# Weight parts stored once and loaded ready-made: a change to a hybrid decoder trunk on one Trainium2 core

## The chip, the cores and the metric

The kernel runs on one core of one Trainium2 chip. The metric is device time in microseconds of one execution, lower is better. The engines are TensorE (PE, with its weight loads as PEld), VectorE (DVE), ScalarE (ACT), GpSimd (POOL) and SyncE (SP), which issues nearly all DMAs of this kernel in program order. Each engine works through its own queue in order, and semaphores tie the queues together.

## The reference

One layer of a decoder trunk, for one prompt of 2048 tokens and 8 samples of 8 tokens (2112 token columns in all). Four recurrent mixers of 256 columns each work side by side between two dense projections, and a squared-ReLU channel mixer follows:

```python
h = rmsnorm(x, p['norm1_w']) * (1 + sc1) + sh1
u = jnp.einsum('btd,de->bte', h, p['w_in'])
u_a, u_b, u_c, u_d = split_last(u, IN_SIZES)
...   # y_a: RWKV-7, y_b: gated linear attention, y_c: gated delta net, y_d: SSD
y = jnp.concatenate([y_a, y_b, y_c, y_d], -1) @ p['w_out']
x = x + gt1 * y
h = rmsnorm(x, p['norm2_w']) * (1 + sc2) + sh2
f = jnp.square(jax.nn.relu(h @ p['w_up'])) @ p['w_down']
x = x + gt2 * f
```

The model width is 1024, the hidden width 4096; `w_in` is padded to 32 column tiles of 128. A last RMSNorm gives the output, and the mixers' states are outputs too.

## The kernel before

**Dense products.** All dense products keep float32 accuracy with three reduced-precision products: weights and activations are split into a high part (the value rounded to the engine's float32r type) and a low part (what is left), and `mm3` (lines 117 to 119) adds hi x hi, hi x lo and lo x hi in PSUM. `wload` makes the weights' parts. It works by half tiles of [128, 512]: a DMA on SP brings the raw half (`wr`, four buffers, line 99), ACT casts it to `wh` (three buffers, line 100), and the subtraction that gives `wl` (three buffers, line 102) runs in turn on GpSimd and DVE, on DVE alone in the two large blocks. A half tile then serves 4 x 3 products for each token tile.

**How often each weight is read.** The input projection (`stage_A`) runs over the tokens in four passes of 320, 2 x 360, 2 x 360 and 352 columns, and reads all 64 half tiles of `w_in` in each. The output projection (`F_out`), the up projection (`F_up`) and the down projection (`F_down`) run over four blocks: two small ones of 352 and 360 columns, numbered 0 and 1, and two large ones of 2 x 350 columns, numbered 2 and 3. `SMALL` is the number of small blocks, 2. Each small block reads 16 half tiles of `w_out`, 64 of `w_up` and 64 of `w_down`. So with one token tile a half serves 12 products, with two it serves 24.

**What runs beside them.** The mixers work on eight chunks of 256 prompt tokens and, once, on the samples. They run in two lanes. Their work is many small operations: short products in PSUM tiles named `psm`, convolutions by `conv_silu` (line 698 on DVE), triangular solves (lines 510 to 543), norms. They read the projected columns `u` back from DRAM (line 1915) and store their results `yd` (line 1922). A scheduler lays out each engine's queue ahead of time: the mixers' instructions come first wherever they are ready, the dense stages fill in. Input passes 1 to 3 and the two small blocks run beside the mixers, the two large blocks after them. So a mixer product that waits on DVE holds up the dense products behind it in PE's queue, and a dense product that waits for a weight part holds up the mixers.

Of the kernel before, what the change touches and what calls it, by code (L numbers as in the profile page):

```python
# [8 lines left out]
F32 = mybir.dt.float32  # L9
# [19 lines left out]
WR, WH, WL = 4, 3, 3  # L29
# [7 lines left out]
class Dense:  # L37
    def __init__(self, es, tc, io):
# [8 lines left out]
        self.a_rstd = {}  # L47
        nc.scalar.preload_act_table_set("exp_and_others")
# [10 lines left out]
    def phase(self, pool, width, temps=4, xs=6, lo_eng=None):  # L59
        """Working tiles of the dense stages come from this pool, `width` tokens wide."""  # L60
        self.sb, self.W, self.temps, self.xs = pool, width, temps, xs
        self.lo_eng = lo_eng or [self.nc.vector]
# [25 lines left out]
    def act(self, tags, w, bufs=1):  # L88
        """High and low parts of activations [128, 8, w]; tags: one each."""
        return [self.sb.tile([128, KT, w], F32R, tag=tag, name=self.n(tag), bufs=bufs) for tag in tags]  # L90

    def wload(self, src):
        """A weight tile in two halves, each as a high and a low part."""
        nc, out = self.nc, []
        for h in range(2):
            raw = self.wp.tile([128, 512], F32, tag="wr", name=self.n("wr"), bufs=WR)
            hi = self.wp.tile([128, 512], F32R, tag="wh", name=self.n("wh"), bufs=WH)
            lo = self.wp.tile([128, 512], F32R, tag="wl", name=self.n("wl"), bufs=WL)
            self.w_dma = nc.sync.dma_start(raw, src[:, h * 512 : h * 512 + 512]).ins.name
            nc.scalar.copy(hi, raw)  # L100
            self.lo_i += 1
            self.lo_eng[self.lo_i % len(self.lo_eng)].tensor_tensor(out=lo, in0=raw, in1=hi.bitcast(F32), op=ALU.subtract)  # L102
            out.append((hi, lo))
        return out

    def after_w(self, dma):
        """Keep a load behind the last weights in the queue."""
# [3 lines left out]
    def mm3(self, ps, w, ks, first=True, last=True):  # L111
        """ps += W^T X from high and low parts: hi*hi + hi*lo + lo*hi."""
# [8 lines left out]
    def project(self, src, xs, tag="d"):  # L121
        """PSUM tiles of W^T X for one column tile of a [1024, .] weight; xs: (n, hi, lo) per token tile."""
        w = self.wload(src)
# [7 lines left out]
    def ada(self, raw, halves, psum, tmp):  # L131
        """Modulation vectors [128, 48, 9]; raw(), halves(): two [128, 512] halves for weights and for sums, psum(): a PSUM tile, tmp: [128, 512]."""
# [22 lines left out]
    def ada_part(self, i):  # L155
        """Weights of input tile i % 8 for the six vectors; each vector is done with its last one. Its input tiles are summed by fours
        in the column groups of the array, whose sums are folded by the products that transpose them."""
# [32 lines left out]
    def rstd_bc(self, s, n):  # L190
        """1/rms per token, on all partitions, from per-partition sums of squares s [128, n]."""
# [25 lines left out]
    def split_cols(self, t0, n):  # L217
        """The sample's columns come first."""
# [22 lines left out]
    def modulate(self, src, r, A, shb, t0, n, hi, lo):  # L241
        """hi + lo = (x / rms) * A + shift, x from DRAM."""
# [24 lines left out]
    def hold(self, tile):  # L267
        """The first tile's input stays on chip."""
# [15 lines left out]
    def stage_A(self, i, store, between):  # L284
        """One pass over the input projection; the next pass's norms are prepared on the way."""
# [9 lines left out]
        for j, ct in enumerate([31] + list(range(31))):  # L295
# [3 lines left out]
            for (t0, n, _, _), ps in zip(acts, self.project(self.io["w_in"][ct], [(n, hi, lo) for _, n, hi, lo in acts])):  # L299
# [11 lines left out]
    def gated_add(self, dst, ps, base, ct, ns, n):  # L311
        """dst += gate * ps, the gate per channel (and per sequence in the sample's columns)."""
# [1855 lines left out]
```

## Time and profile before

| | |
|---|---|
| median of 3 runs | 3463.68 us |
| lowest and highest | 3456.1 and 3464.03 us |
| span of the profiled execution | 3454.3 us |
| mean granted TensorE clock | 0.954 |
| DMA traffic | 411.60 MB, mean 119 GB/s |
| weight half tiles loaded, 256 KB each | 872 |

The profiled execution's own time is given as its span, from the first to the last instruction; the runs' times hold what lies around a span as well. A page's group row reads: line, engine, operation, tiles written and read, shapes, count, then busy microseconds, mean nanoseconds of one, then the engine's idle time just before them and what ended it. A row of waits reads: who waited, for whom, microseconds in total, times, longest. A row by stretch gives for a span of time its length, each engine's busy time with its count, the granted clock, the share of DMA time and the rate. A row of one line's instructions gives the shortest, the median and the longest duration in nanoseconds, and the first and the last start.

### The profile page before, as it was taken

What the parts mean: (1) busy time and instruction counts of PE and PEld (TensorE: products, weight loads), DVE (VectorE), ACT (ScalarE), POOL (GpSimd) and SP (SyncE); (2) the same over time, 40 slices, a digit from 0 to 9 for tenths busy, and PEclk for the clock granted to TensorE, in tenths of its full rate; (3) what the DMA queues carried; (4) which work ended last, traced back from release to release, by engine and by line L of the source; (5) the groups of instructions that cost most, each with busy time, mean ns of one, the idle gap of its engine ahead of it and who ended that gap; (6) DMA issues with size and microseconds to landing.
All of it is one profiled execution on the core that took longest, in us unless ns stands there. A gap on an engine that the chain in (4) does not pass through costs nothing.

```text
span 3454.3 us, 62438 instructions
## 1 busy us (share of the span) xinstructions
PE 3297.9 (95%) x23286; PEld 3024.6 (88%) x23286; DVE 2181.7 (63%) x4739; ACT 1471.0 (43%) x3098; POOL 999.7 (29%) x1034
## 2 busy tenths in 40 slices
PE   8999999899998999999989999997999999999998
PEld 5679887898987988988878888887999999999998
DVE  3437555856668769879879869865334445433345
ACT  3453423434344454454454554544332344332334
POOL 2333334624335346336346336242000000000000
PEclk9999999999999989999988999988999999999999
DMA  9863334423235555333343232355222252222222
GB/s 308 257 188 110 92 100 132 137 82 106 95 104 135 147 127 145 99 113 106 117 129 121 96 121 92 124 156 179 72 68 70 95 192 82 98 68 71 68 70 95
DMA packets 339475, 411.60 MB, mean 119 GB/s; under 512 B 98900, under 2 KB 211684, under 8 KB 339172
## 3 DMA queue, kind: packets, MB, share of 16 engines
q1 hardware_dynamic: 339172, 407.62, 38.2%
q8 instruction: 183, 3.00, 0.4%
q14 instruction: 120, 0.98, 0.1%
HBM read 342.69 MB, written 64.80 MB: 118 GB/s over the span
## 4 chain that ended last, share of the span: by engine, by line
PE 73%; DVE 16%; DMA 4%; issue 3%; ACT 2%; POOL 1%; SPq 1%; DVEq 0%; ACTq 0%; POOLq 0%
PE psd L119 19%; PE psd L118 19%; PE psd L117 19%; DVE t L698 3%; DVE wl L102 2%; PE psm L173 1%; DMA u<-u 1%; DVE Xt L517 1%; DVE X L519 1%; DMA ada<-ada_w 1%; DVE d L248 1%; DVE acc L314 1%; PE pse L118 1%; PE pse L117 1%; PE pse L119 1%
## 5 line engine op out<-in xcount | busy, mean ns | idle before, releaser
L100 ACT CAST wh<-wr 128x512 fp32r<-128x512 f32 x872 | 536.2, 618 | 1049.1 <-PE psd L118 884.6
L119 PE MATMUL psd<-a,wl 128*128 128x360 f32 (+3 forms) x2304 | 783.7, 341 | 26.9 <-DVE wl L102 23.8
L118 PE MATMUL psd<-a,wh 128*128 128x360 f32 (+3 forms) x2304 | 780.4, 339 | 7.2 <-DVE a L257 3.4
L117 PE MATMUL psd<-a,wh 128*128 128x360 f32 (+3 forms) x2304 | 779.3, 339 | 5.3 <-ACT a L253 3.1
L102 DVE TENSOR_TENSOR wl<-wr,wh 128x512 fp32r<-128x512 f32 x584 | 430.5, 738 | 333.6 <-ACT wh L100 325.2
L102 POOL TENSOR_TENSOR wl<-wr,wh 128x512 fp32r<-128x512 f32 x288 | 398.9, 1386 | 704.0 <-ACT wh L100 633.0
L119 PEld LDWEIGHTS psd<-a,wl 128*128 128x128 f32 x2304 | 450.9, 196 | 66.8 <-DVE wl L102 30.5
L117 PEld LDWEIGHTS psd<-a,wh 128*128 128x128 f32 x2304 | 451.1, 196 | 30.2 <-issue 9.6
L118 PEld LDWEIGHTS psd<-a,wh 128*128 128x128 f32 x2304 | 451.0, 196 | 24.2 <-issue 10.0
L314 DVE SCALAR_TENSOR_TENSOR acc<-psd,mod,acc 128x350 f32<-128x350 f32 (+2 forms) x384 | 216.7, 569 | 246.4 <-PE psd L119 245.5
L117 PE MATMUL psd<-hh,wh 128*128 128x350 f32 x1024 | 333.3, 326 | 3.4 <-ACT d L368 3.4
L117 PE MATMUL psd<-fh,wh 128*128 128x350 f32 x1024 | 329.3, 323 | 3.7 <-DVE acc L314 3.7
L118 PE MATMUL psd<-hl,wh 128*128 128x350 f32 x1024 | 332.5, 325 | 0.0
L119 PE MATMUL psd<-fh,wl 128*128 128x350 f32 x1024 | 330.9, 324 | 1.2 <-DVE wl L102 1.0
L119 PE MATMUL psd<-hh,wl 128*128 128x350 f32 x1024 | 331.4, 324 | 0.0
L118 PE MATMUL psd<-fl,wh 128*128 128x350 f32 x1024 | 331.3, 324 | 0.0
L215 POOL TENSOR_TENSOR rsc<-rsc,bias 128x2 f32<-128x2 f32 (+4 forms) x30 | 21.3, 720 | 1004.8 <-ACT rsc L203 1002.7
L117 PEld LDWEIGHTS psd<-hh,wh 128*128 128x128 f32 x1024 | 194.3, 190 | 4.0 <-ACT d L368 4.0
L117 PEld LDWEIGHTS psd<-fh,wh 128*128 128x128 f32 x1024 | 193.0, 189 | 4.7 <-DVE acc L314 4.7
L118 PEld LDWEIGHTS psd<-hl,wh 128*128 128x128 f32 x1024 | 195.2, 191 | 0.1
L119 PEld LDWEIGHTS psd<-hh,wl 128*128 128x128 f32 x1024 | 194.6, 190 | 0.0
L119 PEld LDWEIGHTS psd<-fh,wl 128*128 128x128 f32 x1024 | 192.7, 188 | 1.7 <-DVE wl L102 1.7
(581 smaller groups left out, 5977.8 us busy)
## 6 DMA issues: line engine op xcount, KB each, us to landing
wr<-w_down SPq DMA_DIRECT2D x264, 256.0 KB
wr<-w_in SPq DMA_DIRECT2D x256, 256.0 KB
wr<-w_up SPq DMA_DIRECT2D x256, 256.0 KB
ada<-ada_w SPq DMA_DIRECT2D x96, 256.0 KB
wr<-w_out SPq DMA_DIRECT2D x96, 256.0 KB
u<-uo SPq DMA_DIRECT2D x128, 180.0 KB
u<-u SPq DMA_DIRECT2D x124, 128.0 KB
xp<-xT SPq DMA_DIRECT2D x72, 180.0 KB
```

The source lines that it names most:

```text
L100: nc.scalar.copy(hi, raw)
L102: self.lo_eng[self.lo_i % len(self.lo_eng)].tensor_tensor(out=lo, in0=raw, in1=hi.bitcast(F32), op=ALU.subtract)
L117: nc.tensor.matmul(ps, lhsT=lh, rhs=xh, start=first and i == 0, stop=False)
L118: nc.tensor.matmul(ps, lhsT=lh, rhs=xl, start=False, stop=False)
L119: nc.tensor.matmul(ps, lhsT=ll, rhs=xh, start=False, stop=last and i == len(ks) - 1)
L173: nc.tensor.matmul(ps[h][o : o + 32], lhsT=self.cT[:, k], rhs=w[h], start=(k < 4), stop=(k >= 4))
L215: self.nc.gpsimd.tensor_tensor(out=ap, in0=ap, in1=e.to_broadcast(list(ap.shape)), op=ALU.pow)
L248: nc.vector.scalar_tensor_tensor(out=t[:, ns:n], in0=x[:, ns:n], scalar=A[:, k, 0:1], in1=r[:, ns:n], op0=ALU.mult, op1=ALU.mult)
L314: nc.vector.scalar_tensor_tensor(out=dst[:, ns:n], in0=ps[:, ns:n], scalar=self.mod[:, base + ct, 0:1], in1=dst[:, ns:n], op0=ALU.mult, op ...
L517: nc.vector.tensor_tensor(out=tmp[:, :n, :w], in0=X[:, a:hi, j : j + 1].to_broadcast([128, n, w]), in1=MM[:, j, lo:j].unsqueeze(1).to_broa ...
L519: nc.vector.tensor_tensor(out=X[:, a:hi, lo:j], in0=X[:, a:hi, lo:j], in1=tmp[:, :n, :w], op=ALU.add)
L698: nc.vector.scalar_tensor_tensor(out=y[:, q], in0=uv[:, q, i : i + n], scalar=w(i), in1=y[:, q], op0=ALU.mult, op1=ALU.add)
```

## The change

The high and the low part of a half tile become one tile `w` of [128, 2, 512] with three buffers, in place of `wh` and `wl` with three each. `wload` takes a key. The first time that it meets a key, it makes the two parts as before and then stores the tile, 512 KB, to DRAM; the next times it loads that tile into a `w` buffer in one DMA, with no raw half, no cast and no subtraction. Without a key all is as before.

Keys are given to the input projection in passes 1 to 3 (stored in pass 1, loaded in 2 and 3) and to the output, up and down projections in blocks 0 and 1 (stored in 0, loaded in 1). Pass 0 and the two large blocks have none. That is 64 + 16 + 64 + 64 = 208 stores and 128 + 16 + 64 + 64 = 272 ready-made loads.

```diff
-WR, WH, WL = 4, 3, 3
+WR, WB = 4, 3
...
+        self.kept = {}
...
-    def wload(self, src):
+    def wload(self, src, key=None):
         nc, out = self.nc, []
+        kept = self.kept.get(key)
+        made = []
         for h in range(2):
-            raw = self.wp.tile([128, 512], F32, tag="wr", name=self.n("wr"), bufs=WR)
-            hi = self.wp.tile([128, 512], F32R, tag="wh", name=self.n("wh"), bufs=WH)
-            lo = self.wp.tile([128, 512], F32R, tag="wl", name=self.n("wl"), bufs=WL)
-            self.w_dma = nc.sync.dma_start(raw, src[:, h * 512 : h * 512 + 512]).ins.name
-            nc.scalar.copy(hi, raw)
-            self.lo_i += 1
-            self.lo_eng[self.lo_i % len(self.lo_eng)].tensor_tensor(out=lo, in0=raw, in1=hi.bitcast(F32), op=ALU.subtract)
-            out.append((hi, lo))
+            w = self.wp.tile([128, 2, 512], F32R, tag="w", name=self.n("w"), bufs=WB)
+            if kept is not None:
+                self.w_dma = nc.sync.dma_start(w.bitcast(F32), kept[h]).ins.name
+            else:
+                raw = self.wp.tile([128, 512], F32, tag="wr", name=self.n("wr"), bufs=WR)
+                self.w_dma = nc.sync.dma_start(raw, src[:, h * 512 : h * 512 + 512]).ins.name
+                nc.scalar.copy(w[:, 0], raw)
+                self.lo_i += 1
+                self.lo_eng[self.lo_i % len(self.lo_eng)].tensor_tensor(out=w[:, 1], in0=raw, in1=w[:, 0].bitcast(F32), op=ALU.subtract)
+                if key is not None:
+                    d = self.dram.tile([128, 2, 512], F32, name=self.n("wk"))
+                    nc.sync.dma_start(d, w.bitcast(F32))
+                    made.append(d)
+            out.append((w[:, 0], w[:, 1]))
+        if made:
+            self.kept[key] = made
         return out
...
-    def project(self, src, xs, tag="d"):
-        w = self.wload(src)
+    def project(self, src, xs, tag="d", key=None):
+        w = self.wload(src, key)
...
-            ... self.project(self.io["w_in"][ct], [(n, hi, lo) for _, n, hi, lo in acts])
+            ... self.project(self.io["w_in"][ct], [(n, hi, lo) for _, n, hi, lo in acts], key=("in", ct) if i else None)
...
-                ps, = self.project(self.io["w_out"][ct], [(n, hi, lo)], "e")
+                ps, = self.project(self.io["w_out"][ct], [(n, hi, lo)], "e", ("out", ct) if bi < SMALL else None)
...
-            ... self.project(self.io["w_up"][cc * 4 + j], hs)
+            ... self.project(self.io["w_up"][cc * 4 + j], hs, key=("up", cc * 4 + j) if bi < SMALL else None)
...
-            w = self.wload(self.io["w_down"][cc, c2])
+            w = self.wload(self.io["w_down"][cc, c2], ("down", cc, c2) if bi < SMALL else None)
```

What this does to the queues is shown at three places. The first is SP's queue at the start of block 0's channel mixer, where the accumulator `acc` is loaded. Before (line 99 loads a raw half, line 1922 stores a mixer's result):

```order
L392 DMA acc_20000<-x2d 128x8x352
L99 DMA wr_20093<-w_up 128x512
L1901 DMA u_5_259<-uo_17447 128x352
L1905 DMA u_p<-uo_17447 128x3
L99 DMA wr_20129<-w_up 128x512
L99 DMA wr_20135<-w_up 128x512
L1922 DMA yd_269<-yN_12689 128x2x256
L99 DMA wr_20171<-w_down 128x512
L99 DMA wr_20177<-w_down 128x512
```

Now (line 104 loads a raw half, line 110 stores a made tile `w` to its place `wk` in DRAM):

```order
L403 DMA acc_19504<-x2d 128x8x352
L110 DMA wk_19519<-w_19514 128x1024
L1912 DMA u_5_259<-uo_16951 128x352
L1916 DMA u_p<-uo_16951 128x3
L110 DMA wk_19556<-w_19551 128x1024
L104 DMA wr_19603<-w_up 128x512
L104 DMA wr_19640<-w_up 128x512
L110 DMA wk_19563<-w_19558 128x1024
L104 DMA wr_19647<-w_up 128x512
```

Each raw load has a store of twice its size beside it, and the store of a half stands behind its own raw load and three later ones, since it waits for the subtraction.

The second is SP's queue in block 1, a little behind the load of its accumulator. Before (line 1915 loads a mixer's columns `u`):

```order
L99 DMA wr_23574<-w_down 128x512
L1915 DMA u_17983<-u_4_144 128x160
L1915 DMA u_17983<-u_5_145 128x96
L1915 DMA u_17983<-u_4_150 128x160
L1915 DMA u_17983<-u_5_151 128x96
L99 DMA wr_23608<-w_down 128x512
L99 DMA wr_23614<-w_down 128x512
```

Now (line 101 loads a ready-made tile, line 1926 a mixer's columns):

```order
L101 DMA w_23066<-wk_19695 128x1024
L101 DMA w_23096<-wk_19736 128x1024
L1926 DMA u_18324<-u_5_103 128x256
L1926 DMA u_18324<-u_5_109 128x256
L1926 DMA u_18334<-u_5_115 128x256
L1926 DMA u_19288<-u_5_217 128x256
L1926 DMA u_19288<-u_5_223 128x256
L101 DMA w_23098<-wk_19743 128x1024
```

The load of a weight now goes straight into the buffer that PE reads and waits for PE's last product on that buffer; the mixers' loads stand between such loads.

The third is PE's queue around the mixers' last product. Before, it stands in the output projection of block 2 (350 columns), with 8332 of the 14976 dense products ahead of it:

```order
L119 MATMUL psd_26642<-a_4776_26247,wl_26632 128x350
L117 MATMUL psd_26642<-a_4776_26247,wh_26631 128x350
L713 MATMUL psm_19741<-ident,u_19738 128x128 x4
L118 MATMUL psd_26642<-a_4777_26248,wh_26631 128x350
L119 MATMUL psd_26642<-a_4776_26247,wl_26632 128x350
```

Now it stands in the up projection of block 1 (360 columns), with 7546 ahead:

```order
L130 MATMUL psd_24320<-a_3820_22823,w_24316 128x360
L128 MATMUL psd_24320<-a_3820_22823,w_24316 128x360
L724 MATMUL psm_19245<-ident,u_19242 128x128 x4
L129 MATMUL psd_24320<-a_3821_22824,w_24316 128x360
L130 MATMUL psd_24320<-a_3820_22823,w_24316 128x360
```

786 dense products have moved from beside the mixers to behind them.

More of the change, by code (lines that the diff above doesn't have):

```diff
@@ L298, in stage_A @@
                 self.norm_A(*A_PASSES[i + 1][j == 22])
-            for (t0, n, _, _), ps in zip(acts, self.project(self.io["w_in"][ct], [(n, hi, lo) for _, n, hi, lo in acts])):
+            for (t0, n, _, _), ps in zip(acts, self.project(self.io["w_in"][ct], [(n, hi, lo) for _, n, hi, lo in acts], key=("in", ct) if i else None)):
                 o = self.d2("uo", 2)
@@ L364, in F_up @@
             fh, fl = ftile(j)
-            for (t0, n), ps in zip(tiles, self.project(self.io["w_up"][cc * 4 + j], hs)):
+            for (t0, n), ps in zip(tiles, self.project(self.io["w_up"][cc * 4 + j], hs, key=("up", cc * 4 + j) if bi < SMALL else None)):
                 o = t0 - b0
```

## The prediction

> **What bounds the kernel now.** I read the page first (busy shares, slices, chain), then the busy times by stretch, then who waits for whom.
>
> ```profile
> span 3454.3 us, 62438 instructions
> PE 3297.9 (95%) x23286; PEld 3024.6 (88%) x23286; DVE 2181.7 (63%) x4739; ACT 1471.0 (43%) x3098; POOL 999.7 (29%) x1034
> PE 73%; DVE 16%; DMA 4%; issue 3%; ACT 2%; POOL 1%; SPq 1%; DVEq 0%; ACTq 0%; POOLq 0%
> ```
>
> PE is busy 95% of the span and carries 73% of the chain that ended last; VectorE (DVE) has the next 16%. PE's work stays what it is, so the change can only move the 156 us in which PE is idle, and the time that PE spends at a lower granted clock. Where these lie:
>
> ```profile
> core 0: us, PE busy (x) PEld busy (x) DVE busy (x) ACT busy (x) POOL busy (x), PEclk, DMA share, GB/s
> 0.00:240.00 240.00, 228.04 (x1256) 157.82 (x1256) 93.06 (x207) 100.12 (x216) 78.42 (x109) 1.00 0.79 256
> 240.00:635.00 395.00, 385.62 (x2841) 342.94 (x2840) 253.82 (x675) 154.51 (x365) 151.29 (x169) 0.95 0.41 114
> 635.00:1060.00 425.00, 411.99 (x3362) 374.55 (x3361) 291.50 (x692) 183.48 (x405) 156.28 (x173) 0.96 0.35 105
> 1060.00:1310.00 250.00, 230.45 (x1794) 206.50 (x1792) 190.41 (x436) 116.40 (x253) 113.41 (x112) 0.92 0.54 138
> 1310.00:1790.00 480.00, 451.39 (x3510) 408.37 (x3507) 414.51 (x979) 235.69 (x499) 228.97 (x216) 0.93 0.38 119
> 1790.00:2370.00 580.00, 530.04 (x3955) 478.32 (x3954) 469.78 (x958) 279.72 (x587) 252.35 (x236) 0.90 0.38 123
> 2370.00:3454.00 1084.00, 1060.40 (x6580) 1056.12 (x6580) 468.58 (x798) 401.08 (x776) 19.01 (x23) 0.99 0.27 90
> ```
>
> The rows are about the stages: input passes 0, 1, 2 and 3 (the last with the first block's output projection), channel mixer of block 0, of block 1, and of the two large blocks. I call **lost** the idle time of PE plus its busy time times the missing clock. Passes 1 and 2 lose 9.4 + 0.05 x 385.6 = 29 us and 13.0 + 0.04 x 412.0 = 29 us, 7% of each, with DVE busy 64% and 69%. The next three lose 19.6 + 18.4 = 38 (15%, DVE 76%), 28.6 + 31.6 = 60 (13%, DVE 86%) and 50.0 + 53.0 = 103 us (18%, DVE 81%). The last stretch is nearly all PE, and its weights take the same route as before: nothing to win there.
>
> **What the change takes away.** Of the 872 half tiles, 272 are now loaded ready-made: 128 in input passes 2 and 3, and 16 + 64 + 64 of the output, up and down projections of block 1. Each drops a cast and a subtraction, the latter in turn on DVE and GpSimd (POOL):
>
> ```profile
> L100 ACT CAST wh<-wr 128x512 fp32r<-128x512 f32 x872 | 536.2, 618 | 1049.1 <-PE psd L118 884.6
> L102 DVE TENSOR_TENSOR wl<-wr,wh 128x512 fp32r<-128x512 f32 x584 | 430.5, 738 | 333.6 <-ACT wh L100 325.2
> L102 POOL TENSOR_TENSOR wl<-wr,wh 128x512 fp32r<-128x512 f32 x288 | 398.9, 1386 | 704.0 <-ACT wh L100 633.0
> ```
>
> That is 272 x 0.618 = 168 us of ACT, 136 x 0.738 = 100 us of DVE and 136 x 1.386 = 188 us of POOL. None of it is PE time, so what counts is PE's wait for it, by the waits of PE in 1060:1310 and then in 1790:2370, the two kept stretches with losses:
>
> ```profile
> PE psd L119 <- DVE wl L102: 5.3, 3, 3.0
> ```
> ```profile
> PE psd L119 <- DVE wl L102: 11.0, 9, 3.7
> PE pst L334 <- DMA yp<-yd: 6.7, 5, 1.8
> PE psd L334 <- DMA xp<-yd: 6.2, 6, 2.3
> ```
>
> That is 16.3 us directly. More comes through the mixers: their chains run on DVE, and PE, which takes its queue in order, waits for them. By the table the loss goes from 7% at a DVE share of 69% to about 15% at 81% (the mean of three), 0.68% for each point. In 1790:2370 DVE loses 72 x 0.738 = 53 us and goes from 81% to 72%: 6.1% of 580 is 35 us. In 1060:1310 it loses 32 x 0.738 = 24 us, 76% to 67%: 15 us. Pass 2 is at 7% already: nothing. Of these 50 us, which include the 16.3, I take off the quarter that the two loads of y (12.9 of the 50 idle us of block 1) make up, which stay: **38 us gained**. Bounds: 16 us (the waits on wl alone) and 59 us (both stretches down to 7%).
>
> The order shows the same: behind the mixers' last product stand 786 more dense products than before. The cast's release moves from the second to the third product of a weight tile (one tile now holds both parts), 0.16 us by the starts below; the half tiles in front of it cover that, and with the cover gone it would be 0.16 us a half tile.
>
> **What the kept loads cost.** A ready-made half is 128 x 1024 values, 512 KB, into one of three buffers, issued only when PE has let the buffer go; before, four raw halves lay loaded ahead of three made pairs. The pace of the dense products, 24 starts apart, and loads of 256 KB in the chain:
>
> ```profile
> 2319.78 0.32 PE L118 MATMUL psd<-a,wh 128*128 128x350 f32 x1
> ...
> 2323.69 0.33 PE L118 MATMUL psd<-f,wh 128*128 128x360 f32 x1
> ```
> ```profile
> 1256.07 4.23 DMA wr<-w_in
> 2004.34 2.11 DMA wr<-w_down
> ```
>
> 3.91 / 24 = 0.163 us a product, so a half tile of 12 lasts PE 1.96 us. The trace gives no time for such a load of 512 KB of weights. From the tail's 90 GB/s at a share of 0.27 (333 GB/s at full share) the second 256 KB adds 0.79 us: between 2.9 and 5.0 us. With 0.33 us to issue,
>
> ```profile
> L99 SPq DMA_DIRECT2D wr<-w_down x264: 327/328/1312, 1328.6 to 3425.7; - x132
> ```
>
> a buffer goes round in 0.33 + 2.9 + 1.96 = 5.2 us or 7.3 us, so three give a half every 1.73 us (no wait) or 2.43 us (0.47 us late each time). The mean pace of passes with mixers is slower than either (pass 3: 250 us for 80 halves, 3.1 us), so only runs of dense products are caught. The 4.23 row lies in pass 3; I take a quarter of its 64 halves, 16 x 0.47 = **8 us**, and nothing in block 1, where the 2.11 row lies. Bounds: 0 and 192 x 0.47 = 90 us (all single-tile halves of pass 3 and block 1). Queued behind a load that waits on SP stand the mixers' loads of u and their stores of y; before, SP stood as long for weights:
>
> ```profile
> SPq L99 <- DVE wl L102: 1021.5, 356, 9.2
> SPq L99 <- POOL wl L102: 462.1, 164, 14.5
> ```
>
> **What the stores cost.** 208 stores of 512 KB: 64 in pass 1, 16 and 128 in block 0. In 1310:1790 the 128 are 67 MB, 140 GB/s more on 119, a DMA share of 0.38 + 140/333 = 0.80. That share was met in 0:240 (0.79), where PE idled 12 us in 240, 5%; 5% of 480 us, 24 us, is the upper bound, 0 the lower (a transfer that replaces nothing saves nothing). A buffer must now wait for its store as well: cast 0.62, subtraction 0.74 to 1.39, issue 0.33, store 2.9 to 5.0, at most 7.3 us of the 3 x 3.3 us (480 us for 144 halves) that it has. So I take a quarter of the bound, **6 us**. Pass 1 has two token tiles a half, 3.9 us, and room for all of it.
>
> **Sum**: 38 - 8 - 6 = 24 us off the profiled execution's 3454.3 us span, 3430.3. The three times shown (3456.1 to 3464.0, median 3463.7) lie 2 to 10 us above that span; I add the median's 9.4 us: **3440 us**.
>
> **Rivals.**
>
> *PE starves on kept loads (slower), 0.25.* The point is a load, wait and issue included, of more than two halves, 3.9 us. For it: loads queue on SP behind instructions that wait for DVE or ACT, and the slow row is already 4.23 us for half the bytes. Against: mixer products stretch most halves. Half of the 192 halves at 0.47 us is 45 us; the 128 us of dense products moved behind the mixers (786 x 0.163) at a clock of 0.90 in place of 0.99 lose 12 more; the mixers then wait in PE's order, and I leave half of the gain, 19, with 6 for stores: 45 + 12 + 6 - 19 = +44, 3508 us. The clock is the trace's own: 0.90 where PE idles 9%. [...]
>
> *The stores eat the gain (no change), 0.17.* Bound 24 in place of 6, loads 8, gain 38: -6, 3458 us. For it: a share of 0.80. Against: 0:240 shows PE at clock 1.00 under that share.
>
> *More than the subtractions comes off DVE (faster still), 0.15.* DVE's operations often last far longer than their median while POOL runs:
>
> ```profile
> L698 DVE SCALAR_TENSOR_TENSOR t<-u,cw,t x288: 465/479/1567, 111.7 to 2280.6; 128x256 f32<-128x256 f32 x144
> ```
> ```profile
> L698 DVE SCALAR_TENSOR_TENSOR t<-u,cw,t 128x256 f32<-128x256 f32 x288 | 190.6, 697 | 3.2 <-ACT t L694 2.2
> ```
>
> The mean is 697 against a median of 479 ns. If that excess, 31% of the mean, came from POOL and held for all of DVE's 1620 us from 240 to 2370 us (the sum of five rows), the 188 of POOL's 902 us that go, 21%, would free some 100 us of DVE, as much again as counted: the gain reaches its bound of 59 and pass 1 and 2 give some 10 too: 59 + 10 - 6 = -63, 3401 us. [...]
>
> **Chances and range.** Forecast 0.43, rivals 0.25, 0.17 and 0.15. A measurement of this kernel can tell 0.3%, 10 us, from no change. Faster: 0.40 of the forecast and 0.15, so 0.55; same: 0.16, most of the second rival; slower: 0.29, the first rival and the rest of the second. The range takes in the forecast with its bounds, both rivals beside it, and just past the first one's centre: 3385 to 3510 us.
>
> **What would show it.** Casts x600, subtractions x448 on DVE and x152 on POOL; and, from
>
> ```profile
> HBM read 342.69 MB, written 64.80 MB: 118 GB/s over the span
> ```
>
> written 64.8 + 208 x 0.524 = 174 MB, read 342.7 + 272 x 0.262 = 414 MB. Right: PE's waits for wl in pass 3 and block 1 gone, the granted clock there above 0.92, the DMA share in block 0 near 0.8 with PE idle as before, the mixers' last product some 130 us earlier. Wrong: PE's waits named "DMA w<-wk" adding to over 20 us (first rival), waits for u loads or for the cast in block 0 up by over 15 us (second), or the clock unchanged although DVE is freer (then the mixers' loss does not hang on DVE).

## The result, and the profile after

| | before | after |
|---|---|---|
| median | 3463.86 us | 3545.28 us |
| lowest and highest | 3456.1 and 3470.61 us | 3542.28 and 3552.7 us |
| span of the profiled execution | 3454.3 us | 3544.1 us |

The changed kernel takes 1.0243 times the time of before (95% interval 1.0225 to 1.0262): slower, by about 81 us, and beyond the upper end of the predicted range. The page of the changed kernel first (span, busy times, traffic, shares of the chain that ended last):

```profile
span 3544.1 us, 61891 instructions
PE 3320.8 (94%) x23286; PEld 3033.5 (86%) x23286; DVE 2027.8 (57%) x4603; ACT 1314.6 (37%) x2826; POOL 807.2 (23%) x898
HBM read 413.99 MB, written 173.85 MB: 166 GB/s over the span
PE 71%; DVE 11%; DMA 10%; issue 2%; ACT 2%; POOL 1%; SPq 1%; DVEq 0%; ACTq 0%; POOLq 0%
```

DVE, ACT and POOL all lost the work that the change removes, and the traffic is the forecast one. But PE is idle for 223 us (3544.1 - 3320.8) in place of 156, and DMA has 10% of the chain in place of 4%. Where the time goes, by the busy times by stretch of the changed kernel (length, busy time of each engine, granted clock, DMA share, rate):

```profile
core 0: us, PE busy (x) PEld busy (x) DVE busy (x) ACT busy (x) POOL busy (x), PEclk, DMA share, GB/s
240.00:635.00 395.00, 384.56 (x2840) 339.86 (x2839) 269.75 (x695) 156.37 (x370) 155.24 (x173) 0.96 0.64 198
635.00:1060.00 425.00, 412.60 (x3356) 370.95 (x3355) 258.61 (x665) 147.62 (x336) 118.88 (x143) 0.96 0.49 146
1060.00:1310.00 250.00, 219.48 (x1670) 194.87 (x1669) 159.07 (x396) 82.78 (x184) 76.34 (x87) 0.87 0.75 202
1310.00:1790.00 480.00, 434.68 (x3404) 388.69 (x3403) 379.13 (x937) 217.74 (x475) 200.06 (x201) 0.92 0.73 240
1790.00:2450.00 660.00, 582.09 (x4209) 527.79 (x4208) 384.97 (x904) 216.52 (x470) 159.32 (x166) 0.90 0.60 191
2450.00:3544.00 1094.00, 1060.23 (x6579) 1055.37 (x6578) 483.98 (x807) 394.84 (x780) 19.16 (x22) 0.98 0.28 91
```

Passes 1 and 2 are as before. By the prediction's measure of lost time (idle time of PE plus its busy time times the missing clock), the stretch of pass 3 loses 30.5 + 0.13 x 219.5 = 59 us (38 before), that of block 0 45.3 + 0.08 x 434.7 = 80 (60), that of block 1 77.9 + 0.10 x 582.1 = 136 (103), and the tail 33.8 + 0.02 x 1060.2 = 55 (34). That is 95 us more, against 89.8 us between the two spans. The stretch of block 1 is 80 us longer than the one read before, since that stage ends later, so its border to the tail is a rough one; half of the tail's 21 us is a hundredth of the clock, the last digit of its row. So most of the loss arises from pass 3 to block 1, in the stages that store, load or do both, while the passes that only store (pass 1) or only load (pass 2) with two token tiles a half cost nothing. DVE's share is lower than before in pass 3 (64%, from 76%) and in block 1 (58%, from 81%), and the clock fell all the same, from 0.92 to 0.87, and stayed at 0.90.

Who waits, by the waits of PE over the whole changed kernel, the costliest five (who waited, for whom, total, times, longest):

```profile
PE psd L128 <- DMA w<-wk: 48.5, 39, 5.9
PE psd L345 <- DMA xp<-yd: 25.8, 18, 4.7
PE psd L210 <- DVE ssum L245: 11.1, 1, 11.1
PE psd L130 <- POOL w L107: 11.0, 10, 2.4
PE psd L130 <- DVE w L107: 10.0, 8, 3.6
```

The ready-made loads lead the list. SP's own waits in 1040:1400 show why they are late, in this row:

```profile
SPq L101 <- PE psd L130: 90.7, 42, 7.0
```

SP cannot issue a load before PE has done its last product on one of the three buffers, so a load starts two halves ahead at most. In the chain of waits of 1360:1400 such a load takes about 6 us from issue to landing, and a store twice that:

```profile
1361.14 5.97 DMA w<-wk
...
1373.88 5.75 DMA w<-wk
...
1382.54 12.40 DMA wk<-w
1395.04 0.63 ACT w L105
1395.69 0.70 DVE w L107
```

That 12.40 us store stands in SP's queue right behind the load of block 0's accumulator (1408 KB). What it does is seen in the timeline of 1381:1396 (start, duration, engine, instruction, and in brackets the idle time before it with what ended it):

```profile
1381.89 0.56 SPq L403 DMA_DIRECT2D acc<-x2d  x1
...
1382.54 0.61 SPq L110 DMA_DIRECT2D wk<-w  x1
...
1395.04 0.62 ACT L105 CAST w<-wr 128x512 fp32r<-128x512 f32 x1 [5.24 <-DMA wk<-w]
...
1395.71 0.43 PE L128 MATMUL psd<-a,w 128*128 128x352 f32 x1 [3.20 <-ACT w L105]
```

The cast cannot write into a buffer whose store is still under way; ACT stands for 5.24 us with everything behind it in its queue, and PE stands 3.20 us for the cast. The stretches just after it:

```profile
1389.00:1396.00 7.00, 3.80 (x30) 3.54 (x28) 1.68 (x7) 1.72 (x5) 0.00 (x0) 1.00 1.07 311
1396.00:1403.00 7.00, 6.86 (x41) 5.57 (x41) 6.08 (x20) 3.30 (x9) 1.38 (x1) 0.60 0.88 319
```

The clock, 1.00 in the stretch with the wait, is 0.60 in the 7 us behind it: at this place PE pays twice, 3.20 us idle and then 0.40 x 6.86 = 2.7 us of missing clock. These rows show that the low clock follows the wait; that the wait brings it is not shown.

Over the whole changed kernel ACT's casts stood 31.6 us for stores:

```profile
L105 ACT CAST w<-wr 128x512 fp32r<-128x512 f32 x600 | 369.3, 618 | 771.5 <-PE psd L130 631.0 <-PE pse L130 32.9 <-DMA wk<-w 31.6
```

### The profile page after: what moved, and what is told of

Read it like the earlier page. It is cut to its first block, busy times and chain, and to the rows that moved or that the text cites. A ratio compares the mean times of both kernels' runs of the same rounds, so it can differ in the third digit from the quotient of the medians.

```text
span 3544.1 us, 61891 instructions
## 1 busy us (share of the span) xinstructions
PE 3320.8 (94%) x23286; PEld 3033.5 (86%) x23286; DVE 2027.8 (57%) x4603; ACT 1314.6 (37%) x2826; POOL 807.2 (23%) x898
## 4 chain that ended last, share of the span: by engine, by line
PE 71%; DVE 11%; DMA 10%; issue 2%; ACT 2%; POOL 1%; SPq 1%; DVEq 0%; ACTq 0%; POOLq 0%
PE psd L128 19%; PE psd L130 19%; PE psd L129 18%; DMA w<-wk 4%; DVE t L709 2%; PE psm L184 1%; DMA wk<-w 1%; DMA xp<-yd 1%; DVE w L107 1%; DMA wr<-w_out 1%; DMA u<-u 1%; DVE acc L423 1%; DMA ada<-ada_w 1%; PE pse L129 1%; PE pse L130 1%
## 5 line engine op out<-in xcount | busy, mean ns | idle before, releaser
L128 PE MATMUL psd<-a,w 128*128 128x360 f32 (+3 forms) x2304 | 789.1, 343 | 42.5 <-DMA w<-wk 32.0
L130 PE MATMUL psd<-a,w 128*128 128x360 f32 (+3 forms) x2304 | 783.6, 340 | 17.1 <-POOL w L107 8.6
L129 PE MATMUL psd<-a,w 128*128 128x360 f32 (+3 forms) x2304 | 778.6, 338 | 4.2 <-POOL a L265 2.6
L105 ACT CAST w<-wr 128x512 fp32r<-128x512 f32 x600 | 369.3, 618 | 771.5 <-PE psd L130 631.0
L107 DVE TENSOR_TENSOR w<-wr,w 128x512 fp32r<-128x512 f32 x448 | 322.7, 720 | 377.7 <-ACT w L105 352.7
L128 PEld LDWEIGHTS psd<-a,w 128*128 128x128 f32 x2304 | 451.8, 196 | 83.6 <-DMA w<-wk 35.8
L130 PEld LDWEIGHTS psd<-a,w 128*128 128x128 f32 x2304 | 452.2, 196 | 50.4 <-POOL w L107 19.3
L129 PEld LDWEIGHTS psd<-a,w 128*128 128x128 f32 x2304 | 452.9, 197 | 16.6 <-issue 6.3
L129 PE MATMUL psd<-fl,w 128*128 128x350 f32 x1024 | 331.3, 324 | 1.4 <-DVE fl L382 1.4
L130 PE MATMUL psd<-fh,w 128*128 128x350 f32 x1024 | 331.0, 324 | 1.0 <-DVE w L107 1.0
L128 PE MATMUL psd<-hh,w 128*128 128x350 f32 x1024 | 331.8, 324 | 0.0
L128 PE MATMUL psd<-fh,w 128*128 128x350 f32 x1024 | 329.6, 323 | 1.3 <-DVE acc L325 1.2
L129 PE MATMUL psd<-hl,w 128*128 128x350 f32 x1024 | 330.7, 323 | 0.0
L130 PE MATMUL psd<-hh,w 128*128 128x350 f32 x1024 | 330.3, 323 | 0.0
L107 POOL TENSOR_TENSOR w<-wr,w 128x512 fp32r<-128x512 f32 x152 | 207.6, 1367 | 528.0 <-ACT w L105 424.8
L128 PEld LDWEIGHTS psd<-fh,w 128*128 128x128 f32 x1024 | 193.1, 189 | 2.2 <-DVE acc L325 1.9
L130 PEld LDWEIGHTS psd<-fh,w 128*128 128x128 f32 x1024 | 192.7, 188 | 1.3 <-DVE w L107 1.3
```

The lines of the kernel that those rows point to most:

```text
L105: nc.scalar.copy(w[:, 0], raw)
L128: nc.tensor.matmul(ps, lhsT=lh, rhs=xh, start=first and i == 0, stop=False)
L129: nc.tensor.matmul(ps, lhsT=lh, rhs=xl, start=False, stop=False)
L130: nc.tensor.matmul(ps, lhsT=ll, rhs=xh, start=False, stop=last and i == len(ks) - 1)
```

## The experiments

Each run stands beside runs of the kernel before on the same chip. Differences between two experiments are differences of their ratios times 3460 us; the intervals of such a difference are some 9 to 15 us either way.

| run | what it is | median us | ratio to before, 95% interval |
|---|---|---|---|
| e1_merge_only | merged tile alone | 3474.05 | 1.0054 [1.0029, 1.008] |
| e2_stores_only | merged tile and the 208 stores | 3548.73 | 1.0255 [1.0227, 1.0283] |
| e3_loads_only | merged tile and the 272 loads | 3477.0 | 1.0052 [1.0036, 1.0068] |
| e4_in_only | change for the input projection alone | 3482.65 | 1.0081 [1.005, 1.0113] |
| e5_blocks_only | change for the blocks alone | 3506.93 | 1.0135 [1.0111, 1.0159] |
| e12_loads_five | as e3, loads five deep | 3443.5 | 0.9954 [0.9938, 0.997] |
| e13_pairs_only | control of e12 | 3482.38 | 1.0072 [1.0053, 1.0092] |
| e9_stores_tiny | as e2, stores of 16 KB | 3483.17 | 1.0059 [1.0037, 1.008] |
| e10_stores_wb4 | as e2, four made and two raw buffers | 3655.0 | 1.0554 [1.0532, 1.0575] |
| e11_merge_wb4 | control of e10 | 3563.44 | 1.0289 [1.0263, 1.0316] |
| e14_placebo | before, one 64 KB load issued twice | 3462.61 | 1.0009 [0.9996, 1.0023] |
| e15_free_stores | as many full stores, of a constant | 3481.61 | 1.0063 [1.0044, 1.0082] |
| e20_hold_behind | e15 and a small store that holds the tile | 3490.81 | 1.0078 [1.0049, 1.0107] |
| e21_rows_2kb | as e2, rows of 2 KB | 3550.55 | 1.0267 [1.0235, 1.0299] |
| e22_wait_no_hold | e15, each store waits for the subtraction | 3491.93 | 1.0102 [1.0072, 1.0131] |
| e8_five_buffers | whole change, loads five deep | 3495.71 | 1.0094 [1.0066, 1.0121] |
| e16_in_five_split | input alone, five deep, parts apart | 3488.64 | 1.0072 [1.0052, 1.0091] |
| e17_all_five_split | whole change, five deep, parts apart | 3478.86 | 1.0043 [1.0029, 1.0057] |

### The parts of the change, each alone

Against the changed kernel, e1 keeps nothing, e2 stores but never loads, and e3 stores one tile once, from which all 272 loads read:

```diff
 e1
-        kept = self.kept.get(key)
+        key = None
+        kept = None
 e2
-        kept = self.kept.get(key)
+        kept = None
+        key = None if key in self.kept else key
 e3
-                if key is not None:
+                if key is not None and self.first is not None:
+                    made = self.first
+                elif key is not None:
...
+            self.first = made
```

> High and low part in one tile of three buffers, no weight is stored or loaded ready-made. Kept loads as the cause (PE waits for 512 KB loads that go out only when one of three buffers is free): 3464 us, as before, within 10. Stores as the cause (208 stores of 512 KB crowd the queue and hold the buffers): 3464 us as well. Third theory, the merged tile itself (its buffer comes free one product later, and the queues' order changes): 3500 us or more.

> All 208 stores stay, but every reading casts and subtracts again; nothing is loaded ready-made. Kept loads as the cause: 3464 to 3475 us. Stores as the cause: 3510 us or more, with the loss in block 0.

> Only one weight tile is stored, and all 272 ready-made loads read that tile (so the output and the up and down products of those passes are of a wrong weight); the loads' size, place and waits are those of the change. Kept loads as the cause: 3510 us or more, with PE's waits named w<-wk above 40 us. Stores as the cause: 3450 us or less, since casts and subtractions are gone and the stores too.

The merged tile alone costs 0.54%, 19 us, where the prediction put nothing. The loads come on top at -0.02%: nothing is gained by them, and e3 lies between the two ranges expected of it, so it is neither cause alone. The stores come on top at 2.01%, 70 us, which is nearly all of the loss. The three parts add up to 19 - 1 + 70 = 88 us, against 2.43% or 84 us for the whole change: they add up, with no interplay beyond the intervals.

By stage, e4 gives no key to the output, up and down projections, e5 none to the input projection:

```diff
 e4
-                ps, = self.project(self.io["w_out"][ct], [(n, hi, lo)], "e", ("out", ct) if bi < SMALL else None)
+                ps, = self.project(self.io["w_out"][ct], [(n, hi, lo)], "e")
...
 e5
-            ... self.project(self.io["w_in"][ct], [(n, hi, lo) for _, n, hi, lo in acts], key=("in", ct) if i else None)
+            ... self.project(self.io["w_in"][ct], [(n, hi, lo) for _, n, hi, lo in acts])
```

> Only the input projection stores (64, in pass 1) and loads ready-made (128, in passes 2 and 3). By what e2 and e5 showed (stores cost, and e5 alone 3507 us), the rest to 3545: 3480 to 3505 us. If the 64 stores of pass 1 with two token tiles cost nothing and the loads pay: 3455 us or less.

> The input projection makes its parts at every pass, as before; only the output, up and down projections of blocks 0 and 1 store and load. Kept loads as the cause: about half of the 81 us stay, 3490 to 3510 us, since pass 3 has 64 of the 208 single-tile loads and lost 58 us up to dense product 4608. Stores as the cause: 3520 us or more, since 144 of 208 stores and the shorter pace are in block 0.

Beyond the merged tile the input projection costs 0.27%, 9 us, and the blocks 0.81%, 28 us. The two together (37 us) are less than the whole change beyond the merged tile (1.89%, 65 us), so the parts by stage do not add up as the parts by kind do; the difference of 28 us is wider than its interval (some 17 us), and no run explains it. The 3507 us of e5 also lie in the range expected of the loads as the cause, which e2 and e3 do not bear out.

### The loads: the gain is there, and a wait eats it

If PE's waits for the loads hide a real gain, deeper loading must bring it out. In e12 the raw halves lie in pairs, two buffers of the same size as a made tile, and the ready-made loads use these as well: five buffers in the same memory. As e3, it stores one tile only. The control e13 has the pairs, and neither stores nor loads.

```diff
+                self.kept_i += 1
+                tag, bufs = ("w", WB) if self.kept_i % 5 in (0, 2, 4) else ("wr", 2)
+                w = self.wp.tile([128, 2, 512], F32R, tag=tag, name=self.n("w"), bufs=bufs)
...
+                if pair is None:
+                    pair = self.wp.tile([128, 2, 512], F32R, tag="wr", name=self.n("wr"), bufs=2)
+                raw = pair[:, h].bitcast(F32)
```

> Loads only, as e3 (one tile is stored and read for all, so products of passes 2, 3 and block 1 are of a wrong weight), but the ready-made loads go in turn into the three made tiles and into the room of the raw halves, five deep. If PE's waits for w<-wk (42 us in e3) ate the gain of the casts left out: 25 to 45 us below e13. If leaving out casts gains nothing here: within 10 us of e13.

> Control of e12: raw halves in pairs of one tile, no stores, no ready-made loads. About e1 (3474 us), up to 3500 us if the pairs come free too late.

PE's waits for the ready-made loads, in e3 and then in e12:

```profile
PE psd L131 <- DMA w<-wk: 42.1, 29, 4.6
```
```profile
PE psd L137 <- DMA w<-wk: 7.6, 3, 3.0
```

Five buffers take 34.5 us of waits away. Against its control e12 is 1.18% or 41 us faster, the gain that the prediction called 38, while e3 against e1 gains 1 us. So **loading three deep in place of five costs about 40 us** by the two controls, and the rows of PE's waits have 34.5 us of it. The order differs as well: e12 has 8093 dense products ahead of the mixers' last product, e3 7848, with that product at 2225.4 and 2227.1 us. How much the waits alone cost is therefore argued, not shown.

### The stores: which property of them costs 70 us

A store adds bytes, a wait of SP for the subtraction, a hold on the buffer until it has landed, and another order of instructions. e9 has wait and hold, with few bytes (16 of the 512 columns of each part); e15 has all the bytes, from a constant tile `nb`, with neither wait nor hold:

```diff
 e9
-                    nc.sync.dma_start(d, w.bitcast(F32))
+                    nc.sync.dma_start(d[:, :, 0:16], w[:, :, 0:16].bitcast(F32))
 e15
-                    nc.sync.dma_start(d, w.bitcast(F32))
+                    put = nc.sync.dma_start(d, self.plain.rearrange("p a b -> p (a b)").unsqueeze(1).to_broadcast([128, 2, 512]))
+                    ...   # in the order beside the weights, without a wait
```

> Stores only, as e2 (3549 us), but each store writes 16 of 512 columns of each part (1/32 of the bytes), with the same count, place and waits. If the stores cost by their bytes (a buffer held until 512 KB have left it, and other transfers behind them): 3470 to 3485 us, as e1 (3474). If they cost by standing on SP's queue with a wait for the subtraction: 3530 us or more.

> Stores only, as e2 (3549 us), with the same 208 places and 512 KB each, but the bytes come from a constant tile, so that no buffer of weights is held and no store waits for a subtraction. If the crowded DMA queue costs (loads of raw halves and of u land later): 3530 us or more. If the buffer held until its store has landed costs: 3475 to 3490 us, as e1 and e9.

Beyond the merged tile they cost 0.05% and 0.09%, 2 and 3 us, both within the intervals. So neither 109 MB of stores beside the other traffic nor SP's wait with a short hold is dear by itself. A deeper rotation was the next idea, four made tiles paid for with two raw buffers (e11 without stores, e10 with):

```diff
-WR, WB = 4, 3
+WR, WB = 2, 4
```

> Stores only, as e2, with four buffers for the made tile in place of three (and two for the raw half in place of four, for room). If the buffer held by its store is what costs: 40 us or more below e2, that is within 35 us of e11. If the crowded queue costs: within 20 us of the distance that e2 keeps to e1, so 55 to 95 us above e11.

> Control of e10: no stores and no ready-made loads, four buffers for the made tile and two for the raw half. As e1 (3474 us) if two raw halves are enough ahead; up to 3520 us if they are not. What counts is e10 against it.

The two raw buffers cost 2.35%, 81 us, by themselves, and the stores on top 2.65%, 92 us, far from the 35 us at most that were expected if the hold is the cause. With two raw buffers it is another kernel, so the 92 cannot be set beside the 70. But ACT's casts wait for stores in the whole of e10 only this long, and the stores are no cheaper for it:

```profile
ACT w L106 <- DMA wk<-w: 1.5, 1, 1.5
```

What does differ is the order: 7572 dense products stand ahead of the mixers' last product in e10, 8160 in e11. A change of order alone was tried by issuing one small load of before twice, which lets the scheduler lay out the queues anew:

```diff
+        nc.sync.dma_start(self.ident, io["c_ident"])
```

> The kernel before with one small load (64 KB, the identity matrix) issued twice at the start: nothing else differs but the order that the scheduler then finds. If the order is neutral: 3464 us within 5. If the kernel before has a lucky order: 5 to 25 us more, and then the 16 us of e1 need no other cause.

At 1.0009 it is no change. One other order is thus harmless; but it has 8332 dense products ahead of the mixers' last product, just as before, so it does not clear the order that the stores bring.

If the hold is dear by itself, a small store of the made tile queued right behind each of e15's large ones must bring the cost back, if it lands only after them:

```diff
+                    e = self.dram.tile([128, 2, 16], F32, name=self.n("wt"))
+                    nc.sync.dma_start(e, w[:, :, 0:16].bitcast(F32))
```

> e15 (3482 us: 512 KB from a constant tile, no buffer held) with a small store of the made tile right behind each large one in the same queue. The small store cannot land much before the large one ahead of it, so the buffer is held about as long as by a full store. If holding the buffer for a full store's time is the cause: 3525 us or more. If it is something in the full store's own bytes (its source or its packets): 3480 to 3500 us.

It did not: 0.24%, 8 us, beyond the merged tile. Yet ACT's casts stand longer for a tile that is held, in the waits of ACT in e20 than in those of e2:

```profile
ACT w L106 <- DMA wt<-w: 48.4, 27, 4.3
```
```profile
ACT w L106 <- DMA wk<-w: 29.1, 19, 5.3
```

In e9, whose stores are as small but have no large ones ahead of them, no wait of a cast for its store is among the 37 costliest rows of ACT's waits, the least of which is 7.7 us: so behind a large store in e20 the small one held its tile for longer. The theory that the casts' wait for the hold is the price falls. What e2 has and e20 lacks is rows of 4 KB, and the full 512 KB sent after SP's wait. e21 gives e2's DRAM tile another layout (396054 DMA packets in place of 369429, about one more for each of the 208 x 128 rows), which leaves the order of all instructions as it was in e2; e22 is e15 with a real wait:

```diff
 e21
-                    d = self.dram.tile([128, 2, 512], F32, name=self.n("wk"))
-                    nc.sync.dma_start(d, w.bitcast(F32))
+                    d = self.dram.tile([2, 128, 512], F32, name=self.n("wk"))
+                    nc.sync.dma_start(d.rearrange("a p b -> p a b"), w.bitcast(F32))
 e22
-                    ... mybir.DependencyInfo(mybir.DependencyClass.NoSync, mybir.DependencyReason.SCHED_ONLY)
+                    ... mybir.DependencyInfo(mybir.DependencyClass.Sync, mybir.DependencyReason.DATA)
```

> The stores alone again (no tile is loaded back), with the wait for the subtraction, the hold of the tile and the order of the instructions on every engine exactly as in e2; only the DRAM tile is laid out by parts, so that a store goes out in rows of 2 KB instead of 4 KB. If the length of the rows on the queue is what made the stores dear, this gives what e15 and e20 gave with 2 KB rows, 3480 to 3490 us. If the stores cost by the wait, the hold or the order of the instructions, it stays at e2's 3549 (3535 to 3560).

> As e15 (208 stores of 512 KB in 2 KB rows from a constant tile, nothing loaded back, no weight tile held), but each store now waits on SP for the subtraction of its tile, as in e2. If the cost needs SP to wait and then to send the full 512 KB ahead of what is queued, 3530 to 3550. If it needs the weight tile to be held while the 512 KB go out after the subtraction, this stays near e15, 3480 to 3495. If it needs rows of 4 KB, it stays near e15 as well, and e21 tells the two apart.

The rows are innocent: e21 stays at e2's time. The wait before the full 512 KB is not enough either: e22 costs 0.48%, 17 us, beyond the merged tile, and e21 1.65%, 57 us, more than that. SP's waits at the store for subtractions, in 1310:2400 of e21 and then of e22:

```profile
SPq L111 <- POOL w L108: 69.0, 35, 5.0
SPq L111 <- DVE w L108: 38.9, 17, 7.5
```
```profile
SPq L111 <- POOL w L108: 36.8, 25, 8.6
SPq L111 <- DVE w L108: 30.4, 14, 3.8
```

SP stands there 108 us in the one and 67 in the other. Beside this e21 has the casts' wait for stores, which e22 cannot have, and one of its stores, again the one right behind the accumulator's load in SP's queue, is a long piece of the chain of waits in 1040:2400:

```profile
1396.98 11.43 DMA wk<-w
```

So **most of the stores' cost appears only when the 512 KB leave from the weight tile itself, after the subtraction**. The bytes, SP's wait, and a hold by a small store cost 2 to 17 us each, and the length of the rows changes nothing. The remaining 57 us could come from the hold as it runs, or from the order that the scheduler lays out for a tile so held. The casts' waits speak against the first: 48.4 us in e20, whose stores cost 8 us, and 1.5 us in e10, whose stores cost 92.

The order can be read in the traces. The mixers' last product starts at 2327.6 us in e21 and at 2327.7 in e22. What stands behind it is shown by the busy times from there to the end, of one product in three of the dense ones (low part by high part, line 131 in e21, 133 in e22), in e21 and then in e22 (length, PE, PEld, granted clock, DMA share, rate):

```profile
2327.60:3550.90 1223.30, 757.25 (x2336) 442.55 (x2336) 0.97 0.31 100
```
```profile
2327.70:3499.70 1172.00, 736.77 (x2272) 430.69 (x2272) 0.98 0.30 98
```

The mixers end at the same time, but e21 has 64 x 3 = 192 dense products more behind them (7968 of 14976 stand ahead, in place of 8160), and what is left takes 1223.3 in place of 1172.0 us. Those 51.3 us are the whole difference of these two executions. The cheap runs e9, e15, e20 and e22 all have 8160 ahead, as e1 has; the dear ones have fewer (e2 and e21 7968, e10 7572). And where the order is alike the stores cost nothing: in e2 and e22 the first 4208 dense products stand alike among the mixers' products, up to 4800 they are at most 14 apart, and dense product 5000 starts at 1442.3 us in e2 and at 1441.8 in e22, with 98 stores issued in each.

This points to the order of PE's queue, and away from the hold itself. It is not shown: with fewer dense products in their way the mixers of e21 end no earlier. Either they are bound by chains of their own (before, with 8332 products ahead, they end at 2318.2 us), or the hold delays them. A run with e21's order and no hold was not made.

### Versions meant to keep the gain

e8 is the whole change with e12's five buffers. e16 and e17 keep the high and the low part in tiles of their own as before, store each (256 KB) when it is made, and load five deep; e16 has keys for the input projection alone, e17 all keys.

```diff
 e16, e17
+                if self.kept_i % 5 in (1, 3):
+                    hi, lo = tile("wr", F32R, WR), tile("wr", F32R, WR)
+                else:
+                    hi, lo = tile("wh", F32R, WH), tile("wl", F32R, WL)
...
+                    d = [self.dram.tile([128, 512], F32, name=self.n("wk")) for _ in range(2)]
+                    nc.sync.dma_start(d[0], hi.bitcast(F32))
+                    nc.sync.dma_start(d[1], lo.bitcast(F32))
```

> The whole change (3545 us), with ready-made loads five deep as in e12. If stores and loads are two separate losses: 30 to 40 us less, 3505 to 3515 us. If the loads wait only behind the stores' traffic: 3540 us, no change.

> The input projection alone is stored and loaded; high and low part keep their own buffers as before the change, each is stored as soon as it is made (256 KB), and ready-made loads go five deep (three pairs of made buffers, two pairs of raw ones). By the account so far (no merged tile, no wait of the loads, a store that holds a buffer for less time, in a pass with 3.9 us a half): 3440 to 3460 us. If a hold in pass 1 still costs: 3475 us or more.

> As e16 with the output, up and down projections of blocks 0 and 1 too. By the same account: the loads' gain of about 39 us less what block 0's shorter holds still cost (e2's 75 us, cut by the earlier and smaller stores): 3450 to 3490 us. If stores cost by traffic after all: 3500 us or more.

Five buffers bring the whole change from 1.0243 to 1.0094, some 52 us; the 40 us of the loads alone lie within the interval. Parts in their own tiles bring it to 1.0043. Of e16 3440 to 3460 us were expected; it came to 3489, above the 3475 that were to tell of a hold in pass 1, and yet e17, with more than three times its stores, is no slower. No run explains that. Neither beats the kernel before. Only e12 does, and it stores one tile instead of 208.

## Why the prediction was wrong

**What the change removes and adds: right.** 600 casts (the row above), and the subtractions and traffic as counted, by the groups of instructions of the changed kernel:

```profile
L107 DVE TENSOR_TENSOR w<-wr,w 128x512 fp32r<-128x512 f32 x448 | 322.7, 720 | 377.7 <-ACT w L105 352.7 <-DMA wr<-w_in 5.1 <-DMA w<-wk 2.9
L107 POOL TENSOR_TENSOR w<-wr,w 128x512 fp32r<-128x512 f32 x152 | 207.6, 1367 | 528.0 <-ACT w L105 424.8 <-DMA wk<-w 28.1 <-DMA x2d<-xp 14.9
```

**The gain, 38 us: right in size, 41 measured** (e12 against e13). In the changed kernel it cannot be seen, since other waits took its place. Block 1 shows the exchange, by the waits of PE in 1790:2450, where the waits for subtractions, 11.0 us before, have fallen to 4.1:

```profile
PE psd L128 <- DMA w<-wk: 23.5, 21, 5.9
PE psd L345 <- DMA xp<-yd: 22.7, 15, 4.7
PE psd L130 <- POOL w L107: 3.7, 5, 0.8
...
PE psd L130 <- DVE w L107: 0.4, 1, 0.4
```

The rule behind the term, 0.68% of lost time for each point of DVE's share, does not hold in the changed kernel: pass 3 lost 24% of its stretch (59 of 250) at a DVE share of 64%. It was read from a kernel in which the waits for subtractions led PE's list. The size was right, but the rule is not confirmed by it, and the closeness is in part luck. The table before did not bear the rule out either: block 0 lost less (13%) at a share of 86% than pass 3 (15%) at 76%. The upper bound of 59 us (both stretches down to 7%) comes to about 62 from the table: three quarters of 20.5 + 62.4.

**The step on the kept loads, 8 us, failed: 40 measured.** "I take a quarter of its 64 halves, 16 x 0.47 = 8 us, and nothing in block 1, where the 2.11 row lies": PE waited 39 times, 1.24 us each time (48.5 / 39), and 21 of these times in block 1. The duration was taken from loads of 256 KB in quiet spots and from the mean pace of the halves, while the pieces above show 5.75 and 5.97 us, above the range of 2.9 to 5.0. The bound of 90 us held, though it counted 192 single-tile halves where pass 3 and block 1 have 64 + 144 = 208; the bound is then 98 and the rival's 45 us become 49. The 40 us come from the two controls and take the order of the queue with them. The first rival had the mechanism and its price, and its condition of a load longer than two halves, 3.9 us, is what the chain shows.

**The step on the stores, 6 us, failed and is the largest: 70 measured, beyond its bound of 24.** Its first half, on traffic, was right: a DMA share of 0.73 in block 0 (0.80 was forecast), and full stores that nobody waits for cost 3 us (e15). The second half took a buffer that "must now wait for its store as well: ... at most 7.3 us of the 3 x 3.3 us ..." as the only other price, covered by the mean pace of the halves. Two things were wrong with it. A store can take 12.40 or 11.43 us, not at most 5.0, and PE then stands, as shown above; but PE's waits for casts in block 0 of the changed kernel come to 6.7 us in all, so this direct wait is a small part of the 70. And no term was given to what the stores do to the order of PE's queue, where the 51.3 us between the executions of e21 and e22 show. Why the stores bring that cost stays open. The bound itself was taken from a stage without such stores (0:240), so it could only bound the traffic. (The 3.3 us divide the stretch of block 0's channel mixer by 144 halves; it has 128, which gives 3.75 us and still more room.)

**The merged tile, put at nothing: 19 us measured.** "The half tiles in front of it cover that, and with the cover gone it would be 0.16 us a half tile." 19 us over 872 half tiles is 0.02 us each: the cover is good, not whole. That the later release of the cast is the cause was argued, not tested; the order changed too, with 8160 dense products ahead of the mixers' last product in e1 and 8332 before.

The sum, with the measured terms in place of the forecast ones: -41 + 40 + 70 + 19 = +88 us, against -24 forecast and 84 measured by the ratio (the first two are e3's -1, parted by the five buffers). Each cost term was read as covered, wholly or for the most part, by the mean pace of a stage; none came out so.

**The step on the order failed too.** "The order shows the same: behind the mixers' last product stand 786 more dense products than before" took the new order as a sign of gain: the mixers were to end some 130 us earlier, and the 786 products are 128 us of PE. The mixers' last product came 100 us earlier, by this row of the changed kernel's line 724 (before: 2318.2):

```profile
L724 PE MATMUL psm<-ident,u x96: 270/273/476, 395.9 to 2218.1; 128*128 128x128 f32 x96
```

What stands behind it, by the same one product in three of the dense ones, before (line 119) and then in the changed kernel (line 130):

```profile
2318.20:3454.30 1136.10, 717.17 (x2215) 419.33 (x2215) 0.98 0.29 95
```
```profile
2218.10:3544.10 1326.00, 804.45 (x2477) 470.13 (x2477) 0.97 0.34 109
```

The 262 x 3 = 786 products more take 190 us more, not 128. They run at the end of block 1 and at the start of block 2, where the granted clock of 2218.1:2410 is 0.90 and PE is busy for 154.6 of 191.9 us, by these waits above all:

```profile
PE psd L345 <- DMA xp<-yd: 21.4, 14, 4.7
PE psd L128 <- DMA w<-wk: 7.8, 9, 3.2
```

190 less 100 is 90 us, the whole difference of the two spans. Only the first rival charged anything for these products, 12 us for the clock.

**Of the other signs named ahead**: PE's waits for subtractions are gone from pass 3 (5.3 us before), but the clock there fell to 0.87. PE idled more in block 0 than before (45.3 us against 28.6), and the waits on "DMA w<-wk" passed 20 us, the sign of the first rival. Of the second rival's sign there is a part: ACT's casts stood 28.9 us for stores in block 0, but PE's own waits for casts there are the 6.7 us above. The third rival, a gain through POOL, finds no support: POOL is busy 803.9 us in e12 and 999.3 in e13, 20% less, and e12 gains what was forecast without that. In the trace of before, of the 288 operations in the rival's row the 93 that last over 600 ns all overlap an instruction of POOL, and the 102 that overlap none last at most 488 ns. But that POOL is the cause, and with it the rival's 100 us of DVE, no run shows: in the changed kernel, with POOL busy 807.2 us in place of 999.7, the same operations (line 709) last 698 ns on average, as against 697 before.

## What to carry to other kernels

The work taken off ACT, DVE and POOL gained 41 us here with ready-made loads five deep (e12), and 1 us with loads three deep (e3), for which PE waited 42.1 us: count the buffers that a prefetch may fill ahead of its reader, and set the load's duration under the traffic of that stage against the fastest run of products, not against the mean pace. Test the parts of a store apart: here the bytes cost 3 us, and the same bytes out of an operand's own buffer 70, with another order of the queues. And where a scheduler lays out the queues, an edit can change their order as well: the merged tile alone took the dense products ahead of the mixers' last product from 8332 to 8160. Read from the trace when the chain beside the dense work ends and how many dense products are left then, since a difference there can be the whole difference in time, as the 51.3 us between e21 and e22 were.

## What the runs showed that was not expected

- Rows of 4 KB and of 2 KB in the stores give the same time: 3548.73 and 3550.55 us (e2 and e21, with the same order of instructions).
- 109 MB of additional stores beside a kernel that is bound by PE cost 3 us when nothing waits for them (e15 against e1), at a DMA share of 0.73 in 1310:1790:

```profile
1310.00:1790.00 480.00, 443.13 (x3424) 401.89 (x3423) 401.29 (x937) 225.34 (x479) 220.70 (x205) 0.91 0.73 247
```

- A store of 512 KB issued right behind the 1408 KB load of the accumulator took 12.40 us in the changed kernel, where the loads of 512 KB before it took about 6, and 11.43 us in e21.
